# Turning a decoder's inner activations by transposing transfers of 16-bit halves instead of on TensorE

## The chip, the core and the metric

The kernel runs on one core of a Trainium2 chip. The metric is device time in microseconds (us) of one execution, taken as the median of several. A core has five engines that run their own instruction queues in order: TensorE (PE, matrix products, with its weight loads shown as PEld), VectorE (DVE), ScalarE (ACT), GpSimd (POOL) and SyncE (SP, which here only starts transfers). SBUF is the working memory with 128 partitions, PSUM the memory that TensorE writes its results to, in banks of 512 32-bit numbers a partition.

## The reference

One token sequence of 256 goes through two layers of width 2048. Layer 0 is a retention layer with 8 heads, layer 1 an attention layer with shared keys and values; each is followed by a squared-ReLU MLP with 8192 inner features. The parts that the change touches, cut:

```python
def retention(h, w_in, w_out, cos, sin):
    ...
    o = o * lax.rsqrt(jnp.mean(o * o, axis=-1, keepdims=True) + RMS_EPS)
    o = o.reshape(b, s, H * dv).astype(h.dtype)
    return (jax.nn.silu(gate) * o) @ w_out

def sq_relu_mlp(h, w1, w2):
    return jnp.square(jax.nn.relu(h @ w1)) @ w2

    for layer in range(DEPTH):
        ...
        x = x + sq_relu_mlp(rms_norm(x, norm_mlp[layer]), mlp_w1[layer], mlp_w2[layer])
```

## The kernel before

**Matrix products in halves.** TensorE multiplies 32-bit numbers in a shortened format. So every operand is split in two: a high half, which ScalarE makes by a cast (`split`, L216), and a low half, the rest, which VectorE makes by a subtraction (L217). Each product is three matmuls of 128x512: high by high, high by low, low by high (`mm`, L409 to L411). The weights come from HBM in chunks of 1 MB (`raw`, 3 buffers, issued on SP's queue), each split in parts of 1024 columns (`wh` and `wl`, 5 buffers each), which ScalarE and VectorE make in turn ahead of TensorE.

**Pairs with seven products.** `gemm_pair` takes a chunk (`quad`) of two 128-row blocks against 1024 columns. Plain chunks need 8 products in two parts (24 matmuls). Chosen chunks (the tuples `SEVEN`, `ODD`, `LATE`, `HEAD`) need 7 in four parts (21 matmuls), for which VectorE first adds weight blocks (`u`, L363 to L373) and the activations' sums (`with_sums`, L455 to L459). At the end `pair_out` copies six accumulators out of PSUM on ScalarE (L432) and `summed` (L448) adds them on VectorE.

**The MLP.** `mlp` works through four groups of 2048 inner features. In each, two "up" gemms (`u0_0`, `u0_1`, ...: layer, number) make 1024 inner features each, 8 chunks long, and two "down" gemms (`d0_00`, `d0_01`, ...) bring the group back to 2048 columns. A result of an up gemm lies token-major: 128 tokens on the partitions, 512 features along. As the left operand of the down gemm it must be feature-major. So `up` takes four 512-wide columns c (two token tiles by two halves), applies the Relu with the norm's scale (L877), and `turn` turns them: `transposed` (L235) has TensorE do four 128x128 transposes against an identity into a PSUM bank for each block of 256 features, ScalarE squares the bank into SBUF (`u`, L886), and the block is split like any operand (`hid`). Every second block also gets its sums.

**Retention.** For each head `ret_out` makes a gated, normed output y of two token tiles by 512 (L764) and turns it in the same way to two blocks (`yt`), which the later gemms with `ret_w_out` read. Six of the 16 blocks are first copied to SBUF (L774), because they need sums; the others are split straight from PSUM.

**What sets the order.** Each engine has one queue. The kernel's text gives the order in which work is made: `later(n, fn)` puts work n ticks ahead, a tick being one weight chunk, and `need` runs what is due early when an operand is missing. So what an up gemm leaves (copies, Relus, turning, splitting) is made during the first chunks of the next gemm, between its weight casts: that of u0_0 in u0_1, that of u0_1 in d0_00. From what is made, a scheduler then orders each engine's queue by its own estimates, and the queue is fixed before the run.

Of the kernel before, what the change touches and what calls it, by code (L numbers as in the profile page):

```python
# [12 lines left out]
F32R = mybir.dt.float32r  # L13
BF16 = mybir.dt.bfloat16
I32 = mybir.dt.int32
AF = mybir.ActivationFunctionType
ALU = mybir.AluOpType
AX = mybir.AxisListType
# [17 lines left out]
P = 128  # L36
NT = 2
S = NT * P
# [4 lines left out]
RH, RDK, RDV = 8, 256, 512  # L43
# [23 lines left out]
def yoco(ctx: ExitStack, tc: tile.TileContext, a):  # L67
# [4 lines left out]
    def f2k(shape, name, dtype=F32):  # L72
        return pool.tile([P, *shape], dtype, tag="f2k", bufs=14, name=name)
# [149 lines left out]
    def split_act(v, src, scales=(None, None)):  # L223
        if scales == (None, None):
            split(v[:, :, 0], v[:, :, 1], src)
        else:
            for j in range(2):
                split(v[:, j, 0], v[:, j, 1], src[:, j], scales[j])

    def transposed(srcs, name):  # L230

        tp = bank("tp", [2, S], name)
        for j in range(2):
            for t in range(NT):
                nc.tensor.transpose(tp[:, j, t * P : (t + 1) * P], srcs(t, j), ident)  # L235
        return tp

    def stream(w, chunk, cols, name, use, done=None, before=None):

# [211 lines left out]
    def with_sums(blocks, name):  # L451

        blocks = blocks.rearrange("p j (t n) -> p (j t) n", t=NT)
        sums = f2k([4, P], f"{name}_sum")
        nc.vector.tensor_tensor(sums[:, 0:2], blocks[:, 0:2], blocks[:, 1:4:2], op=ALU.subtract)  # L455
        nc.vector.tensor_tensor(sums[:, 2], sums[:, 1], blocks[:, 0], op=ALU.subtract)
# [291 lines left out]
    def ret_out(h, s, v, gate, y_act):  # L748
        o = two_banks(f"o{h}")
        ys = []  # L750
        for t in range(NT):
            for m in range(t + 1):
                lo = m * S + (t - m) * P
                sh, sl = (i[:, lo : lo + P] for i in s)
                vh, vl = v[m]
                nc.tensor.matmul(o[:, t], sh, vh, start=m == 0, stop=False)
                nc.tensor.matmul(o[:, t], sh, vl, start=False, stop=False)
                nc.tensor.matmul(o[:, t], sl, vh, start=False, stop=m == t)
        for t in range(NT):
            so = small(1, f"so{h}{t}")  # L760
            square_sum(o[:, t], so, f"o{h}{t}")
            ro = rstd(so, RDV, 1, f"o{h}{t}")
            y = f2k([512], f"y{h}{t}")
            nc.vector.scalar_tensor_tensor(y, o[:, t], ro, gate[t], op0=ALU.mult, op1=ALU.mult)  # L764
            ys.append(y)

        def turn():
            for k2 in range(2):
                tp = transposed(lambda t, j: ys[t][:, (2 * k2 + j) * P : (2 * k2 + j + 1) * P], f"ytp{h}{k2}")
                yt = act_tile(f"y{h}{k2}")  # L770
                more = None
                if len(y_act) in (HEAD if h < RH // 2 else LATE):
                    u = f2k([2, S], f"yu{h}{k2}")
                    nc.scalar.copy(u, tp)  # L774
                    split_act(yt, u)
                    more = with_sums(u, f"y{h}{k2}")
                else:
                    split_act(yt, tp)
                y_act.append((yt, more))

        later(2 if h else 3, turn)

# [81 lines left out]
    def mlp(layer, act, r, done):  # L864
        w1, w2 = a[f"mlp_w1_{layer}"], a[f"mlp_w2_{layer}"]
        f0 = 0
        for gi, nf in enumerate(GROUPS):
            hid, blocks = [], []
            last = gi == len(GROUPS) - 1

            def up(c, p, hid=hid, blocks=blocks):

                need(r, NT)
                c = summed(c)
                for t in range(NT):
                    for i in range(2):
                        nc.scalar.activation(c[t][i], c[t][i], AF.Relu, scale=r[t])  # L877

                def turn(i):
                    for q in (2 * i, 2 * i + 1):  # L880
                        name = f"hid{layer}_{p}{q}"
                        tp = transposed(
                            lambda t, j: c[t][q // 2][:, (q % 2 * 2 + j) * P : (q % 2 * 2 + j + 1) * P], f"{name}_tp"
                        )
                        u = f2k([2, S], f"{name}_u")
                        nc.scalar.activation(u, tp, AF.Square)  # L886
                        v = act_tile(name)
                        split_act(v, u)
                        blocks.append((v, with_sums(u, name) if len(blocks) in ODD else None))
                        hid.append(v)  # L890

                later(0, lambda: turn(0))
                later(1, lambda: turn(1))

            for p in range(f0 // 2, (f0 + nf) // 2):
                seven = SEVEN if p % 2 else ODD if p else LATE
                gemm_pair(
                    w1, p * 8, act, [i in seven for i in range(8)], f"u{layer}_{p}", lambda c, p=p, up=up: up(c, p)
                )
# [393 lines left out]
```

## Time and profile before

| | |
|---|---|
| median of 3 runs | 2460.07 us (2459.26 to 2462.01) |
| span of the profiled execution, first to last instruction | 2456.3 us |
| TensorE busy | 2446.2 us, 11614 instructions |
| VectorE busy | 2212.2 us |
| ScalarE busy | 1641.3 us |
| granted TensorE clock | 1.00 throughout |
| moved by DMA | 521 MB, 212 GB/s |

The profiled execution has no time of its own beside its span; the runs' median lies 3.8 us above it. A row of a timeline reads: start, length, engine, line of the kernel, operation, output <- inputs, shape, count; rows of one kind that follow each other are merged. The square bracket behind a row says how long the engine was idle before it and what ended that. Starts of consecutive instructions on one engine lie closer than their lengths, because each is drained while the next begins. A row of the table of busy times by stretch gives the length, then busy time and count of PE, PEld, DVE, ACT and POOL, the clock, the DMA share and GB/s. In the groups the names have lost their numbers: `u_wh` stands for the high halves of all up gemms.

### The profile page before, as it was taken

What the parts mean: (1) busy time and instruction counts of PE and PEld (TensorE: products, weight loads), DVE (VectorE), ACT (ScalarE), POOL (GpSimd) and SP (SyncE); (2) the same over time, 40 slices, a digit from 0 to 9 for tenths busy, and PEclk for the clock granted to TensorE, in tenths of its full rate; (3) what the DMA queues carried; (4) which work ended last, traced back from release to release, by engine and by line L of the source; (5) the groups of instructions that cost most, each with busy time, mean ns of one, the idle gap of its engine ahead of it and who ended that gap; (6) DMA issues with size and microseconds to landing.
All of it is one profiled execution on the core that took longest, in us unless ns stands there. A gap on an engine that the chain in (4) does not pass through costs nothing.

```text
span 2456.3 us, 31721 instructions
## 1 busy us (share of the span) xinstructions
PE 2446.2 (100%) x11614; PEld 2057.6 (84%) x11614; DVE 2212.2 (90%) x2919; ACT 1641.3 (67%) x2307; POOL 238.0 (10%) x287
## 2 busy tenths in 40 slices
PE   9999999999999999999999999999999999999999
PEld 7888888888888888888888888998888888888887
DVE  7899899888899999999999998777899999999998
ACT  6566666556676767667676777577667667676674
POOL 6400001000000010010110001101000100100100
PEclk9999999999999999999999999999999999999999
DMA  8555569556565586695786555444555865957854
GB/s 309 207 201 191 192 202 259 191 183 224 197 218 194 196 254 218 207 272 187 241 253 213 200 202 180 155 162 173 197 199 205 252 228 194 262 198 229 264 209 170
DMA packets 93692, 521.05 MB, mean 212 GB/s; under 512 B 11104, under 2 KB 12512, under 8 KB 40288
## 3 DMA queue, kind: packets, MB, share of 16 engines
q1 hardware_dynamic: 72144, 472.83, 55.2%
q0 software_dynamic: 21248, 46.15, 8.9%
q8 instruction: 91, 1.49, 0.2%
q14 instruction: 65, 0.53, 0.1%
q10 hardware_dynamic: 144, 0.05, 0.0%
HBM read 479.14 MB, written 39.85 MB: 211 GB/s over the span
## 4 chain that ended last, share of the span: by engine, by line
PE 92%; DVE 2%; ACT 1%; issue 0%; DMA 0%; POOL 0%; ACTq 0%; DVEq 0%
PE u_c L411 7%; PE u_c L410 7%; PE u_c L409 7%; PE d_c L411 6%; PE d_c L410 6%; PE d_c L409 6%; PE rp_c L411 3%; PE rp_c L409 3%; PE rp_c L410 3%; PE u_p L411 2%; PE u_p L410 2%; PE u_p L409 2%; PE rq_acc L307 2%; PE rk_acc L307 2%; PE ro_c L411 2%; PE ro_c L409 2%
## 5 line engine op out<-in xcount | busy, mean ns | idle before, releaser
L217 DVE TENSOR_TENSOR d_wl<-d_raw,d_wh 128x1024 fp32r<-128x1024 f32 (+1 forms) x256 | 278.7, 1111 | 31.6 <-ACT d_wh L216 31.6
L217 DVE TENSOR_TENSOR u_wl<-u_raw,u_wh 128x1024 fp32r<-128x1024 f32 (+1 forms) x256 | 279.3, 1113 | 29.8 <-ACT u_wh L216 29.8
L409 PE MATMUL u_c<-u_wh,n 128*128 128x512 f32 x712 | 278.3, 392 | 0.0
L411 PE MATMUL u_c<-u_wh,n 128*128 128x512 f32 x712 | 277.2, 389 | 0.0
L410 PE MATMUL u_c<-u_wl,n 128*128 128x512 f32 x712 | 277.2, 389 | 0.0
L409 PE MATMUL d_c<-d_wh,hid 128*128 128x512 f32 x706 | 275.4, 392 | 0.5 <-ACT d_wh L216 0.5
L411 PE MATMUL d_c<-d_wh,hid 128*128 128x512 f32 x706 | 275.0, 390 | 0.0
L410 PE MATMUL d_c<-d_wl,hid 128*128 128x512 f32 x706 | 274.8, 389 | 0.0
L216 ACT CAST u_wh<-u_raw 128x1024 fp32r<-128x1024 f32 (+1 forms) x256 | 241.3, 973 | 49.6 <-PE u_c L411 24.1
L216 ACT CAST d_wh<-d_raw 128x1024 fp32r<-128x1024 f32 (+1 forms) x256 | 240.3, 971 | 39.9 <-PE d_c L411 16.6
L216 ACT CAST d_wh<-d_u 128x1024 fp32r<-128x1024 f32 x106 | 108.1, 1051 | 119.7 <-DVE d_u L373 82.6
L216 ACT CAST u_wh<-u_u 128x1024 fp32r<-128x1024 f32 x104 | 106.2, 1052 | 116.0 <-DVE u_u L373 77.3
L411 PEld LDWEIGHTS u_c<-u_wh,n 128*128 128x128 f32 x712 | 133.7, 188 | 27.8
L410 PEld LDWEIGHTS u_c<-u_wl,n 128*128 128x128 f32 x712 | 133.8, 188 | 27.4 <-DVE u_wl L217 0.3
L409 PEld LDWEIGHTS u_c<-u_wh,n 128*128 128x128 f32 x712 | 133.7, 188 | 27.0
L409 PEld LDWEIGHTS d_c<-d_wh,hid 128*128 128x128 f32 x706 | 132.6, 188 | 28.2 <-ACT d_wh L216 1.4
L411 PEld LDWEIGHTS d_c<-d_wh,hid 128*128 128x128 f32 x706 | 132.5, 188 | 27.6
L410 PEld LDWEIGHTS d_c<-d_wl,hid 128*128 128x128 f32 x706 | 132.6, 188 | 27.5 <-DVE d_wl L217 0.4
L216 ACT CAST rp_wh<-rp_raw 128x1024 fp32r<-128x1024 f32 x112 | 103.8, 945 | 74.2 <-PE rp_c L411 49.2
L217 DVE TENSOR_TENSOR rp_wl<-rp_raw,rp_wh 128x1024 fp32r<-128x1024 f32 x112 | 119.7, 1090 | 16.4 <-ACT rp_wh L216 16.2
L217 DVE TENSOR_TENSOR u_wl<-u_u,u_wh 128x1024 fp32r<-128x1024 f32 x104 | 123.5, 1222 | 3.1 <-ACT u_wh L216 2.8
L217 DVE TENSOR_TENSOR d_wl<-d_u,d_wh 128x1024 fp32r<-128x1024 f32 x106 | 125.8, 1221 | 0.0
(570 smaller groups left out, 6505.3 us busy)
## 6 DMA issues: line engine op xcount, KB each, us to landing
u_raw<-in_mlp_w SPq DMA_DIRECT2D x128, 1024.0 KB, 5.4
d_raw<-in_mlp_w SPq DMA_DIRECT2D x128, 1024.0 KB, 4.9
rp_raw<-in_ret_w_gv SPq DMA_DIRECT2D x56, 1024.0 KB, 4.8
ro_raw<-in_ret_w_out SPq DMA_DIRECT2D x32, 1024.0 KB, 4.9
uq_raw<-in_mla_w_uq SPq DMA_DIRECT2D x24, 768.0 KB, 4.3
rq_raw<-in_ret_w_qk SPq DMA_DIRECT2D x16, 1024.0 KB, 4.9
rk_raw<-in_ret_w_qk SPq DMA_DIRECT2D x16, 1024.0 KB, 4.8
xh<-d_c POOLq DMA_DIRECT2D x48, 256.0 KB, 6.1
```

The costliest lines, as they stand in the source:

```text
L216: nc.scalar.copy(h, src)
L217: return nc.vector.tensor_tensor(l, src, h.bitcast(F32), op=ALU.subtract)
L307: nc.tensor.matmul(acc[f], wh[:, cols], a.rearrange("p i s -> p (i s)"), start=k == 0, stop=k == nk - 1)
L409: nc.tensor.matmul(dst, ah, bh, start=n == 0, stop=False)
L410: nc.tensor.matmul(dst, ah, bl, start=False, stop=False)
L411: nc.tensor.matmul(dst, al, bh, start=False, stop=n == total[key] - 1)
```

## The change

TensorE no longer turns the MLPs' inner activations and retention's output. Instead:

- `turn_by_dma`: ScalarE copies a 128x512 tile of 32-bit numbers, seen as 1024 numbers of 16 bits, so that all first halves come ahead of all second halves (`h`, new L247). Then two transposing transfers, issued on ScalarE's queue, turn each set of halves into a feature-major tile (`t`, new L249). Four transfers of 128 KB and two copies serve two blocks.
- `joined`: for each block ScalarE copies the turned halves into the even and the odd 16-bit places of a 32-bit tile (new L256, two copies of 512).
- The MLP's Square (new L906) then works in place on that tile. The Relus of the second pair of columns are now made with their own turn.
- All y blocks now go through such a tile, and joining, squaring and splitting are put off by a tick or more (`later(1 + i + k2, ...)`, `later(1 + k2, ...)`).

```diff
+    def halves_of(v):
+        return v.bitcast(U16).rearrange("p (n two) -> p two n", two=2)
+
+    def turn_by_dma(blocks, name):
+
+        turned = [f2k([4, S], f"{name}_t{i}", U16) for i in range(2)]
+        for t in range(NT):
+            parts = f2k([2, 512], f"{name}_h{t}", U16)
+            nc.scalar.copy(parts, halves_of(blocks[t]))
+            for i in range(2):
+                nc.scalar.dma_start_transpose(turned[i][:, :, t * P : (t + 1) * P], parts[:, i])
+        return turned
+
+    def joined(turned, k2, u):
+
+        for i in range(2):
+            dst = halves_of(u.rearrange("p j s -> p (j s)"))[:, i]
+            nc.scalar.copy(dst, turned[i][:, 2 * k2 : 2 * k2 + 2].rearrange("p j s -> p (j s)"))
...
         def turn():
+            turned = turn_by_dma(ys, f"y{h}")
             for k2 in range(2):
-                tp = transposed(lambda t, j: ys[t][:, (2 * k2 + j) * P : (2 * k2 + j + 1) * P], f"ytp{h}{k2}")
...
+                later(1 + k2, lambda k2=k2: join(turned, k2))
...
-                for t in range(NT):
-                    for i in range(2):
+
+                def turn(i):
+                    for t in range(NT):
                         nc.scalar.activation(c[t][i], c[t][i], AF.Relu, scale=r[t])
-
-                def turn(i):
-                    for q in (2 * i, 2 * i + 1):
-                        name = f"hid{layer}_{p}{q}"
-                        tp = transposed(
-                            lambda t, j: c[t][q // 2][:, (q % 2 * 2 + j) * P : (q % 2 * 2 + j + 1) * P], f"{name}_tp"
-                        )
-                        u = f2k([2, S], f"{name}_u")
-                        nc.scalar.activation(u, tp, AF.Square)
-                        v = act_tile(name)
-                        split_act(v, u)
-                        blocks.append((v, with_sums(u, name) if len(blocks) in ODD else None))
-                        hid.append(v)
+                    turned = turn_by_dma([c[t][i] for t in range(NT)], f"hid{layer}_{p}{i}")
+                    for k2 in range(2):
+                        later(1 + i + k2, lambda k2=k2: square(turned, i, k2))
+
+                def square(turned, i, k2):
+                    name = f"hid{layer}_{p}{2 * i + k2}"
+                    u = f2k([2, S], f"{name}_u")
+                    joined(turned, k2, u)
+                    nc.scalar.activation(u, u, AF.Square)
+                    v = act_tile(name)
+                    split_act(v, u)
+                    blocks.append((v, with_sums(u, name) if len(blocks) in ODD else None))
```

How the queues stand, at the second up gemm of layer 0, whose chunks are u_10 to u_17, while it digests the first one's results (columns u_0_c). First ScalarE before, from the first cast of chunk u_12 to the first cast of u_13; `wh` are the weights' high halves, `hid_00` and `hid_01` the first two turned blocks:

```order
L216 CAST u_12_wh_7147<-u_12_raw 128x1024
L216 CAST u_12_wh_7163<-u_12_raw 128x1024
L877 ACTIVATE u_0_c_6999<-u_0_c_6999,n_r 128x512
L877 ACTIVATE u_0_c_6995<-u_0_c_6995,n_r 128x512
L877 ACTIVATE u_0_c_6993<-u_0_c_6993,n_r 128x512
L886 ACTIVATE hid_00_u<-hid_00_tp 128x512
L886 ACTIVATE hid_01_u<-hid_01_tp 128x512
L216 CAST hid_00_7064<-hid_00_u 128x2x256
L216 CAST hid_01_7074<-hid_01_u 128x2x256
L216 CAST u_13_wh_7186<-u_13_raw 128x1024
```

The same place now, from the first to the second cast of u_12 (`h` are the rearranged halves, `t` the turned ones):

```order
L217 CAST u_12_wh_7156<-u_12_raw 128x1024
L897 ACTIVATE u_0_c_7035<-u_0_c_7035,n_r 128x512
L249 DMA_TRANSPOSE hid_00_t_7091<-hid_00_h_7093 128x4x128
L249 DMA_TRANSPOSE hid_00_t_7092<-hid_00_h_7093 128x4x128
L247 COPY hid_00_h_7097<-u_0_c_7035 128x1024
L897 ACTIVATE u_0_c_7031<-u_0_c_7031,n_r 128x512
L249 DMA_TRANSPOSE hid_00_t_7091<-hid_00_h_7097 128x4x128
L249 DMA_TRANSPOSE hid_00_t_7092<-hid_00_h_7097 128x4x128
L897 ACTIVATE u_0_c_7029<-u_0_c_7029,n_r 128x512
L247 COPY hid_01_h_7139<-u_0_c_7031 128x1024
L217 CAST u_12_wh_7172<-u_12_raw 128x1024
```

Four issues, two copies and the three Relus have come between the two casts of one chunk (a further copy stands ahead of the first of them). And on to the first cast of u_13, behind two issues more:

```order
L247 COPY hid_01_h_7143<-u_0_c_7029 128x1024
L256 COPY hid_00_u<-hid_00_t_7091 128x512
L249 DMA_TRANSPOSE hid_01_t_7137<-hid_01_h_7143 128x4x128
L249 DMA_TRANSPOSE hid_01_t_7138<-hid_01_h_7143 128x4x128
L256 COPY hid_00_u<-hid_00_t_7092 128x512
L256 COPY hid_01_u<-hid_00_t_7091 128x512
L906 ACTIVATE hid_00_u<-hid_00_u 128x512
L256 COPY hid_01_u<-hid_00_t_7092 128x512
L217 CAST hid_00_7151<-hid_00_u 128x2x256
L906 ACTIVATE hid_01_u<-hid_01_u 128x512
L217 CAST u_13_wh_7209<-u_13_raw 128x1024
```

The joining copies of the first two blocks, which read what the transfers wrote, stand ahead of u_13's first cast. VectorE's queue at this place before; `wl` are the weights' low halves, `u_13_u` the sums of u_13's weight blocks:

```order
L217 TENSOR_TENSOR u_12_wl_7164<-u_12_raw,u_12_wh_7163 128x1024
L457 TENSOR_TENSOR hid_01_sum<-hid_01_u,hid_01_sum 128x128
L363 TENSOR_TENSOR u_13_u_7181<-u_13_raw 128x1024
L217 TENSOR_TENSOR hid_01_more<-hid_01_sum,hid_01_more 128x2x256
L372 TENSOR_TENSOR u_13_u_7182<-u_13_u_7181,u_13_raw 128x512
L455 TENSOR_TENSOR hid_03_sum<-hid_03_u 128x256
```

And now:

```order
L383 TENSOR_TENSOR u_13_u_7204<-u_13_raw 128x1024
L392 TENSOR_TENSOR u_13_u_7205<-u_13_u_7204,u_13_raw 128x512
L393 TENSOR_TENSOR u_13_u_7205<-u_13_u_7205,u_13_raw 128x512
L218 TENSOR_TENSOR u_12_wl_7173<-u_12_raw,u_12_wh_7172 128x1024
L218 TENSOR_TENSOR hid_00_7151<-hid_00_u,hid_00_7151 128x2x256
L475 TENSOR_TENSOR hid_01_sum<-hid_01_u 128x256
L476 TENSOR_TENSOR hid_01_sum<-hid_01_sum,hid_01_u 128x128
L477 TENSOR_TENSOR hid_01_sum<-hid_01_u,hid_01_sum 128x128
L218 TENSOR_TENSOR u_13_wl_7210<-u_13_raw,u_13_wh_7209 128x1024
```

The sums of u_13's weights have moved ahead of u_12's second low half, and the hidden block's low half and sums stand between that and u_13's first low half. On TensorE the transposes between the chunks are gone and nothing else has moved.

More of the change, by code (lines that the diff above doesn't have):

```diff
@@ L15 @@
 I32 = mybir.dt.int32
+U16 = mybir.dt.uint16
 AF = mybir.ActivationFunctionType
@@ L767, in turn, with join @@
         def turn():
+            turned = turn_by_dma(ys, f"y{h}")
             for k2 in range(2):
-                tp = transposed(lambda t, j: ys[t][:, (2 * k2 + j) * P : (2 * k2 + j + 1) * P], f"ytp{h}{k2}")
[L770 to L779, printed above, removed]
+                later(1 + k2, lambda k2=k2: join(turned, k2))
+        def join(turned, k2):
+            u = f2k([2, S], f"yu{h}{k2}")
+            joined(turned, k2, u)
+            yt = act_tile(f"y{h}{k2}")
+            split_act(yt, u)
+            more = with_sums(u, f"y{h}{k2}") if len(y_act) in (HEAD if h < RH // 2 else LATE) else None
+            y_act.append((yt, more))
         later(2 if h else 3, turn)
@@ L867, in mlp, with up @@
         for gi, nf in enumerate(GROUPS):
-            hid, blocks = [], []
+            blocks = []
             last = gi == len(GROUPS) - 1
-            def up(c, p, hid=hid, blocks=blocks):
+            def up(c, p, blocks=blocks):
                 need(r, NT)
                 c = summed(c)
-                for t in range(NT):
-                    for i in range(2):
+                def turn(i):
+                    for t in range(NT):
                         nc.scalar.activation(c[t][i], c[t][i], AF.Relu, scale=r[t])
-                def turn(i):
-                    for q in (2 * i, 2 * i + 1):
-                        name = f"hid{layer}_{p}{q}"
-                        tp = transposed(
-                            lambda t, j: c[t][q // 2][:, (q % 2 * 2 + j) * P : (q % 2 * 2 + j + 1) * P], f"{name}_tp"
-                        )
-                        u = f2k([2, S], f"{name}_u")
-                        nc.scalar.activation(u, tp, AF.Square)
-                        v = act_tile(name)
-                        split_act(v, u)
-                        blocks.append((v, with_sums(u, name) if len(blocks) in ODD else None))
-                        hid.append(v)
+                    turned = turn_by_dma([c[t][i] for t in range(NT)], f"hid{layer}_{p}{i}")
[4 more added lines that the diff above has]
+                    u = f2k([2, S], f"{name}_u")
+                    joined(turned, k2, u)
+                    nc.scalar.activation(u, u, AF.Square)
+                    v = act_tile(name)
+                    split_act(v, u)
+                    blocks.append((v, with_sums(u, name) if len(blocks) in ODD else None))
                 later(0, lambda: turn(0))
```

## The prediction

> **What bounds the kernel now.** I read the page first, then the chain that ended last, then busy times by stretch, then the timelines of TensorE, ScalarE and VectorE over one gemm of the first MLP.
>
> ```profile
> span 2456.3 us, 31721 instructions
> PE 2446.2 (100%) x11614; PEld 2057.6 (84%) x11614; DVE 2212.2 (90%) x2919; ACT 1641.3 (67%) x2307; POOL 238.0 (10%) x287
> ...
> PE 92%; DVE 2%; ACT 1%; issue 0%; DMA 0%; POOL 0%; ACTq 0%; DVEq 0%
> ```
>
> TensorE (PE) is busy all the time and 92% of the chain is its own. So TensorE work that goes is worth its full length, if nothing else becomes late. VectorE (DVE) is at 90%. By gemm (760 to 804 is the second "up" gemm, which also digests the first one's results; 848 to 888 is a "down" gemm with nothing to digest):
>
> ```profile
> 760.00:804.00 44.00, 44.00 (x204) 36.62 (x203) 41.44 (x52) 31.60 (x42) 0.00 (x0) 1.00 0.57 196
> 848.00:888.00 40.00, 40.00 (x178) 33.11 (x178) 37.35 (x40) 24.90 (x29) 6.09 (x7) 1.00 0.82 238
> ```
>
> The columns are length, then busy PE, weight load, DVE, ACT, POOL, then clock and DMA share. In the digesting gemm DVE has 2.6 us to spare in 44 and ScalarE (ACT) 12.4. Sixteen gemms are of this kind (2 layers x 4 groups x 2 up gemms, each digested by the gemm behind it), and all the MLPs' transposes lie in them.
>
> **What goes: TensorE's transposes.**
>
> ```profile
> L235 PE MATMUL hid_tp<-cst,u_c x256: 270/272/273, 770.8 to 2378.3; 128*128 128x128 f32 x128
> ...
> L235 PE MATMUL ytp<-cst,y x64: 270/272/328, 99.9 to 656.9; 128*128 128x128 f32 x64
> ```
>
> ```profile
> 776.91 0.39 PE L411 MATMUL u_c<-u_wh,n 128*128 128x512 f32 x1
> 777.14 1.03 PE L235 MATMUL hid_tp<-cst,u_c 128*128 128x128 f32 x8
> 777.93 0.48 PE L409 MATMUL u_c<-u_wh,n 128*128 128x512 f32 x1
> 778.24 0.40 PE L410 MATMUL u_c<-u_wl,n 128*128 128x512 f32 x1
> 778.48 0.39 PE L411 MATMUL u_c<-u_wh,n 128*128 128x512 f32 x1
> ...
> 783.24 0.39 PE L411 MATMUL u_c<-u_wh,n 128*128 128x512 f32 x1
> 783.47 0.39 PE L409 MATMUL u_p<-u_wh,n 128*128 128x512 f32 x1
> ```
>
> From 778.48 to 783.24 lie 21 matmul steps: 0.227 us each. From 776.91 to 778.24 there are two such steps and eight transposes: 1.33 - 0.45 = 0.88 us for eight. Each digesting gemm has 16, so 1.76 us; 320 in all are 40 x 0.88 = 35.2 us. That is all that can be gained, and it leaves 2425 us.
>
> **What comes: ScalarE's work.** For each pair of blocks: two 1024-wide 16-bit copies, four transposing issues, four 512-wide joining copies; per digesting gemm twice that. Neither a 16-bit copy nor a transposing transfer is in the trace; the nearest rows:
>
> ```profile
> 767.13 2.97 ACT L216 CAST u_wh<-u_raw 128x1024 fp32r<-128x1024 f32 x3
> 769.97 2.22 ACT L877 ACTIVATE u_c<-u_c,n_r 128x512 f32<-128x512 f32 x3
> 772.09 1.06 ACT L886 ACTIVATE hid_u<-hid_tp 128x512 f32<-128x512 f32 x2
> 773.05 1.14 ACT L216 CAST hid<-hid_u 128x512 fp32r<-128x512 f32 x2
> 774.08 1.57 ACT L216 CAST u_wh<-u_raw 128x1024 fp32r<-128x1024 f32 x2
> ```
>
> From start to start ACT takes 2.84 / 3 = 0.95 us for a 1024-wide cast, 0.70 for a Relu, 0.48 for a 512-wide Square, 0.52 for a 512-wide cast. I price a 16-bit copy by its width: 0.95 and 0.48. (Ends: half of it, or as here; an element of half the bytes is no reason for more.) The Squares, casts and low halves behind them keep their widths and only read SBUF where they read PSUM: nothing.
>
> The price of an issue, i, decides the most:
>
> ```profile
> L119 ACTq DMA_DIRECT2D gains<-in_gains x1: 405/405/405, 0.7 to 0.7; - x1
> ...
> DMA to landing us min/median/max: 2.5/2.5/2.5
> ```
>
> ```profile
> L324 SPq DMA_DIRECT2D u_raw<-in_mlp_w x128: 327/328/328, 699.8 to 2345.7; - x128
> ```
>
> ```profile
> L152 POOL DMA_DIRECT2D xh<-d_c x48 | 41.6, 866 | 784.6 <-DVE d_wl L217 439.6 <-ACT d_p L432 229.3 <-DVE u_wl L217 109.2
> ```
>
> A plain issue held ACT 0.405 us: the lower end. If the queue were held until the data has landed, it would be 2.5 us, as for the one transfer that ACT issues: the upper end. A transposing transfer names four blocks in each of 128 rows where a plain one names one run, so I expect well over the plain price, and more than the 0.87 us of POOL, the slowest issuer in the trace: I take 1.2 us, a choice. The Trainium skill, page "VectorE: DVE Perf Modes", section "The three transpose paths", gives 1309 ns for a transposing transfer of one 128x128 16-bit block against 390 ns on TensorE, and advises TensorE where PSUM will do; no row here shows a transfer, TensorE's row is 272 ns. Read as the hold of one issue, its 1.31 would make my sum 2637, an estimate by that page.
>
> **Where it lies.** I walk through the digesting gemm u_1 (chunks u_10 to u_17), with the new order of the queues. VectorE's rows:
>
> ```profile
> 771.32 2.36 DVE L217 TENSOR_TENSOR u_wl<-u_raw,u_wh 128x1024 fp32r<-128x1024 f32 x2
> 773.59 0.42 DVE L455 TENSOR_TENSOR hid_sum<-hid_u 128x256 f32<-128x256 f32 x1
> 773.93 1.30 DVE L217 TENSOR_TENSOR hid<-hid_u,hid 128x512 fp32r<-128x512 f32 x2
> 775.13 0.29 DVE L456 TENSOR_TENSOR hid_sum<-hid_sum,hid_u 128x128 f32<-128x128 f32 x1
> 775.34 1.23 DVE L217 TENSOR_TENSOR u_wl<-u_raw,u_wh 128x1024 fp32r<-128x1024 f32 x1
> ...
> 781.35 1.23 DVE L217 TENSOR_TENSOR u_wl<-u_raw,u_wh 128x1024 fp32r<-128x1024 f32 x1
> ```
>
> Today the low half of u_13's first part (781.35) is ready at 782.58 and needed at 783.69: a lead of 1.1 us, with VectorE never idle since 771. That is all the slack there is on VectorE.
>
> Without transposes TensorE would begin u_11 at 770.79, u_12 at 776.23, u_12's second part at 778.95, u_13 at 781.67 (24 steps a chunk, 12 a part).
>
> *u_12's second part.* ACT starts the cast of u_11's second part at 767.13 as now. Then stand a 16-bit copy (768.08), u_12's first cast (769.03), a Relu (769.98), and from 770.68: two issues, copy 0.95, Relu 0.70, two issues, Relu 0.70, copy 0.95. The cast of u_12's second part, the third of the three from 767.13 today, so at 769.03, then starts at 770.68 + 3.30 + 4i = 773.98 + 4i = 778.8. VectorE can start its low half at 779.8 and ends at 781.1; TensorE wants it with its second matmul at 779.2: 1.9 us late.
>
> *u_13's first part.* From the start of that cast ACT has the cast itself (0.95), four more issues, one copy (0.95), four joining copies (4 x 0.48), two Squares (0.96) and a hidden block's cast (0.52) ahead of it: u_13's cast starts 5.3 + 4i = 10.1 us later, at 788.9. On VectorE the low half of u_13 stands behind the three sums of a hidden block, and these behind the second Square, which ends at 789.0; the sums take 1.0 (0.42, 0.29 and 0.29 above, each waiting for the one before), so the low half starts at 790.1 and is ready at 791.4. TensorE, late by 1.9, wants it at 783.8: 7.6 us late.
>
> *The rest.* VectorE then has hidden blocks and low parts in a row without slack; by its 1.14 us a wide part and 0.60 a narrow one against 12 and 6 steps of TensorE, u_13's next two parts are 0.4 and 0.5 late, and u_15's 0.7 and 0.3. After that it is ahead again.
>
> Sum: 1.9 + 7.6 + 0.4 + 0.5 + 0.7 + 0.3 = 11.4 late, less 1.76 saved: 9.6 us per gemm, x 16 = 154 us. The same walk gives 3.2 us with i = 0.405 (52 us in all), 7.0 with 0.87, 12.8 with 1.6, 20.0 with 2.5 (320 us). Even with i = 0 the late low parts eat the saving (0.1 us).
>
> **Landing.** The first joining copy waits for the third transfer, issued at 774.7, and is reached at 783.1: 8.4 us for it.
>
> ```profile
> xh<-d_c POOLq DMA_DIRECT2D x48, 256.0 KB, 6.1
> ```
>
> These transfers are twice as large and take 6.1 us, so I cost the landing at nothing; at 10 us the walk gives 12.2 instead of 9.6. The weights' loads share the DMA engines with 160 x 128 KB more; SP has room for it:
>
> ```profile
> SPq L324 <- DVE u_wl L217: 620.7, 127, 11.0
> ```
>
> Its loads wait 4.9 us on average for a buffer that VectorE frees, so a load that lands some us later costs nothing; gone, it would stop VectorE directly. Some loads now also wait for a semaphore that they share with a transposing transfer; those are over by then. The halves and the turned blocks take six of the 14 buffers that the columns' copies use too; they are free again before the next gemm's copies come, so I cost that at nothing as well, and if not, those copies wait for a landing.
>
> **Retention.** Eight times: two copies, four issues, four joins less 0.48 in the six blocks that were copied before: 1.9 + 4.8 + 1.9 = 8.6 us, at the start of a head's pair gemm.
>
> ```profile
> 166.54 1.05 ACT L216 CAST rp_wh<-rp_raw 128x1024 fp32r<-128x1024 f32 x1 [1.77 <-PE rk_acc L307]
> ```
>
> There ACT has been waiting for TensorE to free a weight buffer, with all five in use: four parts ahead, 4 x 2.72 = 10.9 us. So the burst is mostly covered. I put 2 us a head for what is not, less 0.88: +9 us in all. Ends: -7 us (all covered) and 8 x (8.6 - 0.9) = +62 (nothing covered).
>
> **Total.** The profiled execution has a span of 2456.3; the runs' median is 2460.07, so 3.8 lie around it or between executions. 2456.3 + 154 + 9 + 3.8 = 2623, as time 2623 us.
>
> **Rivals.**
> 1. *An issue costs what a plain one does* (i near 0.4). For it: the only ACT issue measured took 0.405. The Trainium skill, page "DMA: Bandwidth & Descriptors", section "Issuing engines are not separate DMA queues", says the time to start a DMA is usually small beside the DMA; that plain issue agrees (0.405 of 2.5). Then 52 us, with retention at -7 to +9: 2505 to 2521. Chance 0.14.
> 2. *The queue is held far longer*, or landing becomes the wait, since transposes share engines that are 57% busy: i from 1.6 to 2.5 is 205 to 320 us, with retention 2674 to 2842. Against: nothing in the trace holds a queue so. Chance 0.20.
> 3. *Faster: ACT's lead takes the whole burst.* ACT is at 72% here and idles 12.4 us, and today u_13's cast starts at 774.08, 9.4 us before TensorE gets to u_13. If a 16-bit copy costs half (0.48 and 0.24), what stands ahead of that cast shrinks from 15.3 to 4.5 us with i at 0.2, and TensorE's saving comes through. It decides at i = 0.36, where the walk with half-price copies gives 0; at 0.1 it gives -1.55 us a gemm, at 0.33 -0.2: with retention at -7, 2428 to 2450. Against: every issue row is over 0.32, and a copy's cost has gone by its width. Chance 0.04.
> 4. *The two cancel*: half-price copies with i near 0.4 (+0.4 us a gemm, retention -7), within 5 us of 2460. Chance 0.04.
>
> That the transposes stay on TensorE is no rival: the order has none of the 320 left.
>
> **How the numbers follow.** The forecast, i between 0.87 and 1.6 (111 to 205 us, retention -7 to +62: 2564 to 2727), has 0.58. The range must leave out at most 0.2: it goes from 2505, rival 1's lower end, to 2780, over half of rival 2; left out are rivals 3 and 4 and the upper part of 2. About 0.2% (5 us) is what a measurement can tell here: faster 0.04, same 0.04, slower 0.92.
>
> **What would show it.** Right: TensorE idle some 11 us in each of the 16 digesting gemms, in two pieces, the longer one ended by VectorE's low half of the fourth chunk; ACT's transposing issues about 1.2 us apart; down gemms of the second column half unchanged at 40.8. Wrong: issues of 0.4 us; TensorE still 100% busy; waits ended by the transfers themselves instead of by ACT's queue; retention's heads longer by more than 3 us each.

## The result, and the profile after

| | before | after |
|---|---|---|
| median | 2460.70 us (4 runs, 2459.26 to 2462.01) | 2633.07 us (4 runs, 2624.44 to 2636.55) |
| profiled execution: time, span | span 2456.3 us | 2630.34 us, span 2628.6 us |
| mean granted clock | 1.00 | 0.979 |
| moved by DMA | 521 MB | 542 MB |

The changed kernel is slower: 1.0697 times the time, 95% interval 1.0678 to 1.0717. The forecast of 2623 us was 10 us short.

The page of the changed kernel, its rows on the engines:

```profile
span 2628.6 us, 31496 instructions
...
PE 2483.2 (94%) x11294; PEld 2040.2 (78%) x11294; DVE 2221.8 (85%) x2919; ACT 1801.8 (69%) x2541; POOL 239.7 (9%) x287
```

TensorE lost its 320 transposes and is no longer busy all the time: it is at 94% of a longer span. ScalarE's 1801.8 us do not hold the time that it spends on issues. What TensorE waited for, in the waits' order:

```profile
PE d_c L429 <- ACT d_wh L217: 52.5, 27, 3.8
PE u_p L429 <- ACT u_wh L217: 47.6, 8, 6.7
...
PE rp_p L429 <- DVE st L758: 11.9, 5, 4.8
```

The columns are microseconds in all, times, the longest. ScalarE's casts of weights in the MLPs are what comes too late. The digesting gemms by busy time, each stretch from the first copy of the last gemm's results out of PSUM to the next such copy (the second "up" gemm, then the "down" gemm behind it):

```profile
786.87:838.38 51.51, 45.14 (x188) 35.63 (x187) 39.60 (x50) 39.86 (x55) 0.00 (x0) 0.93 0.58 177
838.38:890.70 52.32, 45.18 (x183) 34.36 (x182) 41.41 (x52) 39.83 (x55) 0.00 (x0) 0.97 0.57 181
```

Before, the same two took 43.3 us each. Now ScalarE has 39.9 us of busy time in each instead of 31.6, TensorE stands idle for 6 to 7 us, and the clock (third number from the end) is no longer 1.00. From the same copies' starts in the timelines, all 16 digesting gemms together take 837.6 us instead of 692.5, so 52.35 each instead of 43.28: 145.1 us. The first MLP gemm's copies begin at 786.87 us, before at 760.78: 26.1 us come from retention. All else is 1.1 us.

ScalarE in the second up gemm. `ACTq` rows are issues on its queue, a row "x2" is two in a row:

```profile
795.72 1.21 ACTq L249 DMA_TRANSPOSE hid_t<-hid_h  x1
...
796.96 1.30 ACTq L249 DMA_TRANSPOSE hid_t<-hid_h  x1
798.30 1.05 ACT L247 COPY hid_h<-u_c 128x1024 uint16<-128x1024 uint16 x1 [1.50 <-issue]
...
799.38 2.55 ACTq L249 DMA_TRANSPOSE hid_t<-hid_h  x2
801.98 0.72 ACT L897 ACTIVATE u_c<-u_c,n_r 128x512 f32<-128x512 f32 x1 [2.00 <-DVE u_u L392]
...
803.54 1.04 ACT L217 CAST u_wh<-u_raw 128x1024 fp32r<-128x1024 f32 x1
803.67 2.54 ACTq L249 DMA_TRANSPOSE hid_t<-hid_h  x2
806.24 1.05 ACT L247 COPY hid_h<-u_c 128x1024 uint16<-128x1024 uint16 x1 [1.66 <-issue]
...
807.32 2.58 ACTq L249 DMA_TRANSPOSE hid_t<-hid_h  x2
809.94 1.38 ACT L256 COPY hid_u<-hid_t 128x512 uint16<-128x512 uint16 x2 [1.98 <-issue]
...
813.37 1.03 ACT L217 CAST u_wh<-u_raw 128x1024 fp32r<-128x1024 f32 x1
...
836.44 2.00 ACT L217 CAST u_wh<-u_u 128x1024 fp32r<-128x1024 f32 x2 [4.15 <-DVE u_u L393]
```

An issue holds the queue for 1.2 to 1.3 us. The first of a pair begins while ScalarE still drains the instruction ahead (803.67, inside the cast that began at 803.54), so the eight issues leave ScalarE idle for 1.50 + 2.00 + 1.66 + 1.98 = 7.1 us, not for the 10.2 that they take. (The 2.00 is put down to VectorE, but it is the two issues of 799.38.) TensorE in the same gemm:

```profile
805.03 0.39 PE L429 MATMUL u_c<-u_wh,n 128*128 128x512 f32 x1
805.90 0.50 PE L430 MATMUL u_c<-u_wl,n 128*128 128x512 f32 x1 [0.48 <-DVE u_wl L218]
...
808.34 0.40 PE L431 MATMUL u_c<-u_wh,n 128*128 128x512 f32 x1
814.45 0.79 PE L429 MATMUL u_p<-u_wh,n 128*128 128x512 f32 x1 [5.72 <-ACT u_wh L217]
815.04 0.63 PE L429 MATMUL u_c<-u_wh,n_more 128*128 128x512 f32 x1
815.84 0.80 PE L430 MATMUL u_p<-u_wl,n 128*128 128x512 f32 x1 [0.16 <-DVE u_wl L218]
```

The gap is in two pieces and where it was forecast: small in the third chunk (at 805), 5.7 us ahead of the fourth chunk, whose first cast is ScalarE's row at 813.37. Behind it a matmul takes 0.63 us instead of 0.39.

### The profile page after: what moved, and what is told of

Its sections match the earlier page's. It is cut to its first block, busy times and chain, and to the rows that moved or that the text cites. A ratio compares the mean times of both kernels' runs of the same rounds, so it can differ in the third digit from the quotient of the medians.

```text
span 2628.6 us, 31496 instructions
## 1 busy us (share of the span) xinstructions
PE 2483.2 (94%) x11294; PEld 2040.2 (78%) x11294; DVE 2221.8 (85%) x2919; ACT 1801.8 (69%) x2541; POOL 239.7 (9%) x287
## 3 DMA queue, kind: packets, MB, share of 16 engines
q8 instruction: 88, 1.44, 0.2%
## 5 line engine op out<-in xcount | busy, mean ns | idle before, releaser
L429 PE MATMUL d_c<-d_wh,hid 128*128 128x512 f32 x706 | 263.3, 403 | 52.8 <-ACT d_wh L217 52.5
L430 PE MATMUL d_c<-d_wl,hid 128*128 128x512 f32 x706 | 286.3, 406 | 6.5 <-DVE d_wl L218 5.2
L431 PE MATMUL d_c<-d_wh,hid 128*128 128x512 f32 x706 | 281.3, 398 | 0.0
L431 PE MATMUL u_c<-u_wh,n 128*128 128x512 f32 x712 | 277.9, 390 | 0.0
L217 ACT CAST u_wh<-u_raw 128x1024 fp32r<-128x1024 f32 (+1 forms) x256 | 243.8, 969 | 42.4 <-PE u_c L431 19.1
L429 PE MATMUL u_c<-u_wh,n 128*128 128x512 f32 x712 | 269.6, 394 | 1.0 <-ACT u_wh L217 1.0
L217 ACT CAST d_wh<-d_raw 128x1024 fp32r<-128x1024 f32 (+1 forms) x256 | 240.8, 964 | 26.8 <-DMA d_raw<-in_mlp_w 10.9
L218 DVE TENSOR_TENSOR rp_wl<-rp_raw,rp_wh 128x1024 fp32r<-128x1024 f32 x112 | 119.8, 1089 | 10.2 <-ACT rp_wh L217 10.1
```

What stands on the lines that cost most here:

```text
L217: nc.scalar.copy(h, src)
L218: return nc.vector.tensor_tensor(l, src, h.bitcast(F32), op=ALU.subtract)
L429: nc.tensor.matmul(dst, ah, bh, start=n == 0, stop=False)
L430: nc.tensor.matmul(dst, ah, bl, start=False, stop=False)
L431: nc.tensor.matmul(dst, al, bh, start=False, stop=n == total[key] - 1)
```

## The experiments

The time of the kernel before beside each was 2460.2 to 2460.5 us. "A gemm" below is the mean of the 16 digesting gemms, from the starts of the first copies out of PSUM in the timelines, as above. A letter (A, B, C, ...) stands for a theory or a rival of the expectations.

| kernel | median us | ratio to before, 95% | a gemm, us |
|---|---|---|---|
| after | 2633.07 | 1.0697 (1.0678 to 1.0717) | 52.35 |
| `split_issues` | 2837.16 | 1.1526 (1.1507 to 1.1545) | 63.2 |
| `wide_issues` | 2546.42 | 1.0349 (1.0326 to 1.0372) | 47.5 |
| `copies_only` | 2474.15 | 1.0056 (1.0041 to 1.0071) | 44.25 |
| `sp_issue` | 2503.82 | 1.0175 (1.0160 to 1.0191) | 45.6 |
| `mlp_only` | 2609.05 | 1.0602 (1.0586 to 1.0618) | 52.7 |
| `spread` | 2606.89 | 1.0592 (1.0575 to 1.0610) | 51.0 |
| `fill` | 2626.18 | 1.0674 (1.0658 to 1.0690) | 52.15 |
| `spread_wide_sp` | 2470.99 | 1.0043 (1.0029 to 1.0058) | 43.8 |
| `ret_later` | 2610.69 | 1.0615 (1.0598 to 1.0631) | 52.4 |
| `hybrid` | 2457.34 | 0.9989 (0.9980 to 0.9998) | 43.05 |

### Is the price of an issue fixed, or does it go by size?

Twice as many transfers of half the size:

```diff
-                nc.scalar.dma_start_transpose(turned[i][:, :, t * P : (t + 1) * P], parts[:, i])
+                for q in range(2):
+                    nc.scalar.dma_start_transpose(
+                        turned[i][:, 2 * q : 2 * q + 2, t * P : (t + 1) * P], parts[:, i, 256 * q : 256 * (q + 1)]
+                    )
```

> Each transposing transfer is cut into two of 256 of its 512 columns (64 KB each); bytes, copies and joins are as in the changed kernel (2633 us, digesting gemms 52.3 us instead of 43.3). Theory A, an issue holds ScalarE's queue for a fixed time of some 1.3 us whatever its size: sixteen issues a gemm instead of eight, the walk goes from 11 to 21 us, so some 10 us more a gemm, 2790 to 2850 us in all, and each half transfer still shows about 1.2 us. Rival B, the hold goes by bytes: half the length each, 2633 us. Rival C, the transfers' landing is what is waited for: about 2633 us, since the bytes are the same.

And half as many of twice the size:

```diff
-        turned = [f2k([4, S], f"{name}_t{i}", U16) for i in range(2)]
+        turned = [f2k([8, P], f"{name}_t{t}", U16) for t in range(NT)]
...
-            for i in range(2):
-                nc.scalar.dma_start_transpose(turned[i][:, :, t * P : (t + 1) * P], parts[:, i])
+            nc.scalar.dma_start_transpose(turned[t], parts.rearrange("p i n -> p (i n)"))
...
```

> One transposing transfer of 1024 columns (256 KB) for each token tile instead of two of 512; copies and joins keep number and width (the joining copy reads its four pieces of 128 in another order). Theory A, a fixed hold of 1.3 us an issue: four issues a gemm instead of eight, the walk loses 5.1 us a gemm, so 2633 - 82 and up to 10 from retention: 2535 to 2560 us. Rival B, the hold goes by bytes: twice the length each, 2633 us. Rival C, landing: 2633 us or above.

Measured 2837 and 2546 us: both inside theory A's ranges, and far from 2633. The issues of the MLPs by line, first with half the size, then as in the change, then with twice the size (min/median/max ns):

```profile
L250 ACTq DMA_TRANSPOSE hid_t<-hid_h x256: 1183/1265/3243, 830.3 to 2752.5; - x128
```

```profile
L249 ACTq DMA_TRANSPOSE hid_t<-hid_h x128: 1205/1297/2200, 795.7 to 2544.2; - x128
...
DMA to landing us min/median/max: 2.4/4.1/9.0
```

```profile
L248 ACTq DMA_TRANSPOSE hid_t<-hid_h x64: 1247/1249/3440, 797.1 to 2469.3; - x64
```

64, 128 or 256 KB: 1.25 to 1.30 us each. What is paid is the number of issues. From 8 to 16 a gemm costs 63.2 - 52.35 = 10.85 us, 1.36 for each; from 4 to 8 it costs 4.85, 1.21 each. ScalarE is busy for 39.9 us a gemm in all three, and idle for other reasons than an issue for 5.2 to 5.8; idle under an issue it is for 17.6, 7.2 and 2.4 us, and the gemm's length follows that.

Landing is not what is waited for in the MLPs. In the changed kernel no wait of ScalarE in the MLPs is put down to a transfer. With half the size 188.8 us of them are, but these are issues too: each ends where the row of the issues ends, here at 855.16:

```profile
850.06 5.10 ACTq L250 DMA_TRANSPOSE hid_t<-hid_h  x4
855.20 1.38 ACT L259 COPY hid_u<-hid_t 128x512 uint16<-128x512 uint16 x2 [4.51 <-DMA hid_t<-hid_h]
```

With twice the size one join of the MLPs does wait for landing (5.7 us), and retention's wait 37.1 us in all instead of 15.0: retention gained nothing there, as the MLP's first copies begin at 788.3 us.

### Issues taken off ScalarE

Without transfers (joins read the rearranged halves, so that nothing is turned; every copy is there):

```diff
-            for i in range(2):
-                nc.scalar.dma_start_transpose(turned[i][:, :, t * P : (t + 1) * P], parts[:, i])
...
-            nc.scalar.copy(dst, turned[i][:, 2 * k2 : 2 * k2 + 2].rearrange("p j s -> p (j s)"))
+            nc.scalar.copy(dst, halves[k2][:, i])
```

> The changed kernel without its transfers: ScalarE makes the same 16-bit copies and joins, but the joins read the rearranged halves directly, so nothing is turned and nothing has to land. Theory A: what is left is the copies' own place in the queue, by the walk some 0 to 2.4 us a gemm (no slow-clock stretch behind a long gap), retention -7 to +10: 2450 to 2510 us. Rival D, the 16-bit copies alone fill ScalarE: over 2560 us. What this run lacks of 2633 is the price of issues and landing together.

With the transfers, on another queue:

```diff
-                nc.scalar.dma_start_transpose(turned[i][:, :, t * P : (t + 1) * P], parts[:, i])
+                nc.sync.dma_start_transpose(turned[i][:, :, t * P : (t + 1) * P], parts[:, i])
```

> The same transfers issued on SyncE's queue, which starts the weights' loads, instead of on ScalarE's; copies, joins and bytes as in the changed kernel. Theory A, the loss is ScalarE's time under issues: as without transfers, 2450 to 2520 us, a little more if the weights' loads queue behind an issue. Rival C, landing carries the loss: 2600 us or above, and the joining copies wait for the transfers. Rival E, the loads of weights, queued behind issues that wait for ScalarE's copies, become late: above 2560 us, with TensorE or the casts waiting for loads of weights.

Measured 2474 and 2504 us, as theory A has it; D, C and E fall. Of the 172 us that the change costs, 129 go when the same transfers are issued elsewhere, and 30 more when they are gone. The second up gemm with the copies alone, by busy time:

```profile
758.36:802.27 43.91, 43.57 (x188) 34.52 (x188) 39.47 (x50) 39.36 (x54) 0.00 (x0) 1.00 0.52 184
```

ScalarE is as busy as in the changed kernel (39.4 us) and the gemm still takes 43.9: the copies fit into it, the issues did not. They are not free either: 44.25 us a gemm is 2.7 over the 41.5 that TensorE needs without transposes, so the copies, with the order of the queues that comes with them, eat the saving. With the issues on SyncE ScalarE comes to the joins sooner and waits for landing, 19.1 us in the MLPs, where it never waited for a transfer before:

```profile
ACT hid_u L256 <- DMA hid_t<-hid_h: 19.1, 14, 2.8
```

### The MLPs alone

```diff
         def turn():
-            turned = turn_by_dma(ys, f"y{h}")
             for k2 in range(2):
-                later(1 + k2, lambda k2=k2: join(turned, k2))
+                tp = transposed(lambda t, j: ys[t][:, (2 * k2 + j) * P : (2 * k2 + j + 1) * P], f"ytp{h}{k2}")
...
```

> The MLPs as in the changed kernel, retention's output turned by TensorE as before. By the trace of the changed kernel the MLPs' digesting gemms carry about 146 us of the 172 and retention 26: 2602 to 2612 us. By the prediction's own terms 2623 - 9 = 2614 us. Rival: retention's share comes out differently because the slow stretches there also disturb what follows: under 2590 or over 2620 us.

Measured 2609 us: the parts add up. Retention costs 2633 - 2609 = 24 us and the MLPs 149, where the forecast had 9 and 154.

### Is it the place in ScalarE's queue, or is ScalarE full?

The same instructions, one token tile's part a chunk:

```diff
-                later(0, lambda: turn(0))
-                later(1, lambda: turn(1))
+                for n, (i, t) in enumerate(itertools.product(range(2), range(NT))):
+                    later(n, lambda i=i, t=t: turn(i, t))
...
-                        later(1 + i + k2, lambda k2=k2: square(turned, i, k2))
+                        later(2 + k2, lambda k2=k2: square(sets[i], i, k2))
```

> The changed kernel with the MLPs' turning spread over the chunks of the digesting gemm: one token tile's Relu, copy and two issues a chunk (four chunks), and each block's join, Square and split one chunk later than the one before, from the fourth on. Same instructions, same issues of 1.3 us on ScalarE, other places in its queue. Theory A, the loss comes from where the burst stands, all ahead of the fourth chunk's first cast: most of the 9 us a gemm goes, 2500 to 2550 us. Rival F, ScalarE is simply full: 31.6 us of its work in a digesting gemm before, plus 4 copies of 0.95, 8 joins of 0.63 and 8 issues of 1.28 are 51 us, as long as the gemm now takes, so the place does not matter: 2600 to 2635 us, with ScalarE at work all through those gemms.

Measured 2607 us. My own theory A falls here, and the time is in rival F's range: with the burst cut in four, a gemm gained 1.3 us of 9. The spread kernel's second up gemm, and the waits of TensorE:

```profile
781.62:833.18 51.56, 46.27 (x188) 36.79 (x187) 39.12 (x50) 39.91 (x54) 0.00 (x0) 0.93 0.67 177
```

```profile
PE d_c L437 <- ACT hid L217: 39.7, 8, 5.3
PE u_c L437 <- ACT u_wh L217: 27.5, 9, 3.8
```

TensorE's gap has moved from the fourth chunk (`u_p`) to later ones (`u_c`), still ended by ScalarE. In the down gemms it now waits for a turned block (`hid`, 39.7 us in all), which the spreading itself makes late; the up gemms have no such wait and still fell from 52.1 to 51.0 us only. ScalarE's busy time is the same 39.9 us. From the timelines of all 16 gemms, the time in which ScalarE was idle under an issue came to 8.5 us a gemm here and 7.2 in the changed kernel (some issues took longer in their new places, up to 4.77 us; why is not shown), and its other idle time went from 5.3 to 2.7 us. So spreading did close idle time of ScalarE, and lost half of that to longer issues: ScalarE is now at work or under an issue for 48.4 of 51.0 us. In the changed kernel the account is 39.9 busy + 7.2 under issues + 5.3 other = 52.4. By it busy time and the idle time under issues, 47.1 us, are alone 3.8 us more than the whole gemm of before; the other 5.3 us are place and order, and this run won back half of them.

### What the slow clock costs

The page's clock digits hide it; over stretches of 1 us in the changed kernel (clock is the third number from the end):

```profile
810.00:811.00 1.00, 0.00 (x0) 0.00 (x0) 0.00 (x0) 1.00 (x2) 0.00 (x0) 1.00 1.34 264
811.00:812.00 1.00, 0.00 (x0) 0.00 (x0) 0.00 (x0) 1.00 (x3) 0.00 (x0) 0.58 0.92 146
...
817.00:818.00 1.00, 1.00 (x4) 0.81 (x3) 1.00 (x2) 1.00 (x2) 0.00 (x0) 0.51 0.00 0
818.00:819.00 1.00, 1.00 (x6) 0.79 (x5) 1.00 (x2) 1.00 (x2) 0.00 (x0) 1.00 0.46 82
```

Some 2.4 us after TensorE's last matmul the granted clock falls to half, and it is back some 3.5 us after TensorE has begun again at 814.45. To keep it up, `fill` gives TensorE 44 transposes of the identity ahead of that chunk:

```diff
+                    if (i, k2) == (0, 1):
+                        keep = bank("tp", [4, P], f"keep{layer}_{p}")
+                        for n in range(44):
+                            nc.tensor.transpose(keep[:, n % 4], ident, ident)
```

> The changed kernel with 44 transposes of the identity (0.11 us each, 4.8 us) put on TensorE ahead of the fourth chunk of each digesting gemm, where it waits 5.7 us; nobody reads them. Theory G, that gap lets the granted clock fall to half and the first 3.6 us behind it run at half speed, 1.8 us a gemm: with the gap filled the clock stays at 1.0 and the time falls by 20 to 30 us, to 2603 to 2613 us, though TensorE has more to do. Rival H, the clock's record does not set the time, or ScalarE's queue sets the end of the stretch anyway: 2628 to 2640 us.

Measured 2626 us, with the mean clock at 0.992 instead of 0.979. That is neither G's 2603 to 2613 nor quite H's, and the two intervals overlap: the half clock costs little here, though 3.5 us at half speed are 1.8 us in that gemm. (By the mean clock some 40 us at half clock are left of 110, so a small price is not ruled out.) The same place in `fill`:

```profile
809.76 4.96 PE L906 MATMUL keep<-cst 128*128 128x128 f32 x44
815.66 0.50 PE L429 MATMUL u_p<-u_wh,n 128*128 128x512 f32 x1 [0.94 <-ACT u_wh L217]
817.05 0.50 PE L430 MATMUL u_p<-u_wl,n 128*128 128x512 f32 x1 [0.89 <-DVE u_wl L218]
...
829.27 0.50 PE L430 MATMUL u_p<-u_wl,n 128*128 128x512 f32 x1 [0.77 <-DVE u_wl L218]
```

At full clock TensorE only gets sooner to low halves that are not ready: VectorE and ScalarE set the end of the stretch.

### Where retention's 24 us come from

In the changed kernel, in the last head's pair gemm (`rp7`), which turns the output of the head ahead of it; ScalarE, then VectorE, then TensorE:

```profile
610.87 3.11 ACTq L249 DMA_TRANSPOSE y_t<-y_h  x2
614.01 1.05 ACT L217 CAST rp_wh<-rp_u 128x1024 fp32r<-128x1024 f32 x1 [2.23 <-issue]
619.24 1.38 ACT L256 COPY yu<-y_t 128x512 uint16<-128x512 uint16 x2 [4.18 <-DMA y_t<-y_h]
...
621.18 1.99 ACT L217 CAST rp_wh<-rp_raw 128x1024 fp32r<-128x1024 f32 x2
```

```profile
621.30 0.69 DVE L218 TENSOR_TENSOR y<-yu,y 128x512 fp32r<-128x512 f32 x1 [4.98 <-ACT y L217]
...
623.72 0.28 DVE L758 TENSOR_TENSOR st<-sc,dec 128x128 f32<-128x128 f32 x1
```

```profile
624.15 0.77 PE L429 MATMUL rp_p<-rp_wh,a0s_more 128*128 128x512 f32 x1 [4.83 <-DVE st L758]
```

The join stands on ScalarE's queue until the last transfer has landed (4.18 us), VectorE stands behind the block that it yields, and by the code the accumulator rp_p takes a PSUM bank of the kind that the scores hold until VectorE's `st` has read them. The test puts the joins one chunk later:

```diff
-                later(1 + k2, lambda k2=k2: join(turned, k2))
+                later(2 + k2, lambda k2=k2: join(turned, k2))
```

> The changed kernel with retention's two joins each put one chunk later (second and third chunk behind the turning instead of first and second); MLPs as they are. In the changed kernel ScalarE's joins there stand 15.0 us in all waiting for transfers to land, in the late heads 4.2 us at once, with the weights' casts behind them, and TensorE then waits 11.9 us. Theory L, retention's 24 us (2633 less 2609 with the MLPs alone) come from that landing wait, not from the length of the burst: a join one chunk later finds its data landed, the waits for transfers go to under 4 us, and 2610 to 2620 us. Rival M, the burst of copies and issues itself (8.6 us a head) is what is too long, or another wait takes the place: 2628 to 2640 us.

Measured 2611 us, theory L's range. ScalarE's idle time ahead of these copies, before and now, in the order changed kernel and `ret_later`:

```profile
ACT yu L256 <- DMA y_t<-y_h: 15.0, 6, 4.2
```

```profile
  DMA y_t<-y_h: 1.1, 2
```

TensorE's wait for `st` is gone from the answer, and the MLP's first copies begin at 765.6 us instead of 786.9. The issues and copies of retention are all still there; what cost time was the landing.

### Towards a better version

`spread_wide_sp`: the MLPs alone, with one transfer a token tile, on SyncE's queue, spread over the chunks.

> MLPs alone, with all three remedies: one transfer of 1024 columns for a token tile, issued on SyncE's queue, and the work spread over the chunks; retention on TensorE as before. Theory A: ScalarE has 31.6 + 8.9 = 40.5 us of work in a digesting gemm, VectorE 41.4, TensorE without transposes 41.5, so a gemm takes 41.5 to 43.3 us: 2430 to 2462 us. Rival F, the copies' places still delay casts as with the copies alone (1 us a gemm), and the loads queue behind issues on SyncE: 2470 to 2500 us.

Measured 2471 us, in rival F's range and not in theory A's. The up gemms are at 42.5 us, the first to fall below 43.3; the down gemms are at 45.1, because in them a turned block is wanted in the fifth chunk and arrives late:

```profile
PE d_c L435 <- ACT hid L217: 17.9, 8, 2.2
```

`hybrid` therefore turns by transfers only what an up gemm digests:

```diff
+                if p % 2:
+                    later(0, lambda: turn_on_pe(0))
+                    later(1, lambda: turn_on_pe(1))
+                    return
```

> The version that the runs point to: only the results that an up gemm digests (eight of sixteen digesting gemms) are turned by transfers, one of 1024 columns a token tile, issued on SyncE's queue and spread over the chunks; those digested in a down gemm, where a block is wanted by the fifth chunk, and retention's output are turned by TensorE as before. With all sixteen so, the up gemms took 42.5 us instead of 43.3 and the down gemms 44.2 to 45.6. Theory: 8 x -0.78 = -6 us, and up to +1.6 from retention's first head as in the other kernels: 2453 to 2457 us. Rival: the eight down gemms or the loads' later places take it back: 2459 to 2465 us.

Measured 2457.34 us over 11 runs, 0.9989 of before (0.9980 to 0.9998), at the upper end of the theory's range. Its second up gemm and the down gemm behind it:

```profile
762.46:804.97 42.51, 41.98 (x185) 34.47 (x184) 38.42 (x48) 39.51 (x55) 0.00 (x0) 1.00 0.65 213
804.97:848.65 43.68, 43.59 (x199) 35.43 (x198) 43.31 (x55) 31.05 (x44) 0.00 (x0) 1.00 0.56 196
```

The up gemms keep their 0.77 us; the down gemms give back 0.1 to 0.6. That is 3 us of 2460: the only version here that isn't slower, and too little to matter.

## Why the prediction was right, and which steps were off

- **TensorE's transposes are worth 1.76 us a digesting gemm.** Not contradicted, and never seen whole: the most that a kernel showed is 43.28 - 42.51 = 0.77 us.
- **An issue costs 1.2 us.** Right: 1.30 at the median. The ground given, four named blocks in each row, is not: two or eight cost the same. The figure quoted from the Trainium skill, "VectorE: DVE Perf Modes", section "The three transpose paths", 1309 ns for one 128x128 block by transfer, agrees with the hold of one issue, but not as a price by block: an issue of eight such blocks took 1.25 us. (The advice quoted beside it stands in the section "Rules for kernel authors" of the same page of the Trainium skill.)
- **Rival 1, the plain price.** Wrong. The rule quoted with it (the Trainium skill, "DMA: Bandwidth & Descriptors", section "Issuing engines are not separate DMA queues", that the time to start a transfer is usually small beside it) does not hold here: 1.30 us against 4.1 to landing, and taking the starts off ScalarE was worth 129 us.
- **Rival 2, a longer hold or landing.** Not the hold: 1.30 us is below its 1.6. Landing is what retention waited for, at a far smaller price than its 205 us.
- **A 16-bit copy costs by its width.** Right for the wide one (1.05 us long, like the cast of 1024). The joining copy was mis-sized: 0.76 us long and 0.63 from start to start, not 0.48. Rival 3, which needed half prices, falls with it.
- **The walk through u_1.** Right in direction and place, for partly wrong reasons. Late by 0.6 us instead of 1.9 in the third chunk, by 5.9 instead of 7.6 in the fourth; a gemm came to +9.07 instead of +9.6. Two errors cancelled: the prices of issue and join were low (with 1.28 and 0.63 the same walk gives 10.9), but the walk counted each issue in full, and the first of a pair runs beside the instruction ahead (7.2 us lost a gemm of 10.4 held). So that the time came so close is in part luck. Of the 10.8 us that a gemm came late by before the saving (11.4 in the walk), 6.9 show as idle time of TensorE, where some 11 were forecast; the others lie under matmuls that the profile counts as busy, some of them at half clock. The longer wait was ended by ScalarE's cast; VectorE's low half, which began 0.16 us behind that cast's end, made TensorE wait 0.16 us more, so the hidden block's sums ahead of that low half cost next to nothing. That the burst's place ahead of the fourth chunk is all that costs was the wrong reading: `spread` moved it and won 1.3 us of 9, and ScalarE's busy time and its idle time under issues alone are 3.8 us over the gemm of before. The down gemms of the second column half, forecast at 40.8, took 40.4 us.
- **The clock.** Not in the prediction. The Trainium skill, "TensorE: Matmul & The Clock Gate", Part 1, has the clock at half after an idle window of about 3.4 us and at full again after as long a busy one. The way back agrees (3.5 us behind the gap); the fall came sooner, 2.4 us into the gap. `fill` shows that it hardly counts here.
- **Landing costs nothing.** Right for the MLPs in the changed kernel, where ScalarE waited for no transfer. (The 12.2 us for a landing of 10 us do not follow from the steps shown: a first join that waits 10 - 8.4 = 1.6 us more gives 11.2.) Wrong for retention.
- **Retention +9 us.** The step that failed: 24 to 26 us, inside the ends of -7 to +62. "The burst is mostly covered" was right, as `ret_later` shows (+4.8 us up to the MLP with the burst as it is, of which 1.6 stand in `mlp_only` too, with retention on TensorE); the wait for the landing of the last transfer, which I had only costed for the MLPs, was not in the step. By the prediction's own sign (heads longer by more than 3 us each) it was wrong for the last three heads: 5.2, 7.4 and 3.8 us.
- **The sum.** 154 + 9 = 163 against 145 + 26 = 171 us in the profiled executions: the MLPs 9 less, retention 17 more.

## What to carry to other kernels

A transposing transfer that is started on a compute engine's queue has a price on that engine, which did not shrink with its size here (64 to 256 KB). Count issues against the engine's idle time in the stretch where they fall, start as few and as large ones as can be, and from a queue on which no computing waits; the larger ones landed later here (5.1 us against 4.1 at the median). An engine that is off the critical path at 72% can be nearly full in one stretch once copies and issues are added, and then moving the work about inside the stretch gains little. A consumer of a transfer that stands in an in-order queue makes everything behind it wait for the landing: put it behind work that is needed anyway.

## What was not expected of the hardware

- A transposing transfer of 64, 128 or 256 KB held ScalarE's queue 1.25 to 1.30 us at the median alike; single ones took up to 4.8 us. On SyncE it was 1.26 us for 128 KB, and for 256 KB 1.44 in `spread_wide_sp` and 1.35 in `hybrid`.
- The first of two issues overlapped the running instruction of the same engine: pairs of 2.54 to 2.58 us left ScalarE idle for 1.66 to 2.00.
- A copy of 512 16-bit numbers into every second place took 0.76 us, a 512-wide 32-bit Square from SBUF 0.62; one of 1024 that reads every second place took 1.05, as a cast of 1024 did.
- A gap of 5.7 us on TensorE halved its clock until 3.5 us behind it; with ScalarE and VectorE late by as much, filling the gap moved the time by only 7 us of 2633, within the two intervals.
